# RWKV-7 units with two heads in turn on the array, and the latent outputs of both directions in one bank for each head

## The chip, the cores and the metric

The kernel runs on one core of a Trainium2 chip. The metric is the device time of one execution in microseconds: 2151.57 us as the median of three runs of the kernel before (2148.89 to 2158.67). A core has engines with instruction streams of their own: TensorE (PE, matrix products, with its weight loads as PEld), VectorE (DVE), ScalarE (ACT), GpSimd (POOL) and SyncE (SP, which issues most loads).

## The reference

Two layers of a hybrid backbone over 256 latent and 256 context tokens of width 1024. Layer 0 mixes with a gated linear recurrence beside windowed attention and has a dense feed-forward part. Layer 1 mixes with S5 (a complex diagonal state space model) beside RWKV-7 in both directions and ends in a choice of 2 of 8 experts. What the change touches is the RWKV-7 recurrence of layer 1, with 8 heads of 64:

```python
def _rwkv7_scan(r, w, k, v, a, b, s0):
    def step(s, inp):
        rt, wt, kt, vt, at, bt = inp
        sa = jnp.einsum('bhij,bhj->bhi', s, at)
        s = s * wt[:, :, None, :] + sa[..., None] * bt[:, :, None, :] + vt[..., None] * kt[:, :, None, :]
        return s, jnp.einsum('bhij,bhj->bhi', s, rt)
    ...
oc_f, sc_f = _rwkv7_scan(rc, dc[0][0], dc[0][1], vc, dc[0][2], dc[0][3], zero)
ol_f, _ = _rwkv7_scan(rl, dl[0][0], dl[0][1], vl, dl[0][2], dl[0][3], sc_f)
oc_b, sc_b = _rwkv7_scan(*[rev(t) for t in (rc, dc[1][0], dc[1][1], vc, dc[1][2], dc[1][3])], zero)
ol_b, _ = _rwkv7_scan(*[rev(t) for t in (rl, dl[1][0], dl[1][1], vl, dl[1][2], dl[1][3])], sc_b)
out_l = finish(ol_f + rev(ol_b), rl, kl, vl, gl)
```

Only the latent outputs are wanted in this layer; the context gives the state with which the latent tokens start.

## The kernel before

The recurrence is worked out in chunks of 64 tokens: four of context and four latent, in two directions. A unit is one chunk in one direction; step i (0 to 7) takes one unit of each direction d, by `SEQ`, and from step 4 on the chunks are latent. The eight heads lie as four pairs p, and within a pair head h takes the partitions 0 to 63 (h = 0) or 64 to 127 (h = 1): `h2(h)` is that slice. Products are small: 64 columns wide, over 64 or 128 rows.

`unit_before` (L1757) makes what of a unit doesn't need the state. It loads X (`uX`), and for latent chunks makes the gram product of each pair and head: 64 rows, 128 columns, four pairs of one head in one bank, two evacuations by VectorE with a mask (into `lk` and `uz`), then the same for the other head (L1782 to 1788). For context chunks the gram is 64x64 and the heads alternate already. `ztr` is a product with a diagonal matrix that gives the keys (`zh`).

`unit_inverse` (L1808) finishes the inverse of the unit's triangular matrix: two rounds of 32x32 products into one bank (`pi`), four pairs of head 0 and its evacuation (`uP`, `uY`), then four of head 1, in each round.

`rwkv_units` (L1830) runs the eight steps. In one step, for both directions: loads of v into the lower half of `vu` and of the state tile (L1873 and on); `pq`, the products of the gram with the state, whose heads alternate; `pz`, the inverse times `pq` (L1887 to 1892), four pairs of head 0 and then four of head 1, with ScalarE copying head 0's half and VectorE head 1's half into `vu`; `ph`, the new state (L1903 to 1909), again head after head, added to the decayed old state by VectorE (`uT`). Then `unit_inverse` of the next step. The outputs of a latent step are written one step later in `outputs` (L1848 to 1862): for each direction and head a bank `po`, and for each of four pairs a product `uz` x `vu` (128 rows) and one of `uRr` x `uT` (the old state, 64 rows) that adds to it; then one evacuation of 64x256 into `rO`, a copy by ScalarE or an addition by VectorE. `PLACE` says which half of the partitions of which of two output tiles a chunk belongs to; the two chunks of a step are always the two halves of one tile.

Beside this a generator of S5 is advanced twice for each step: its blocks of VectorE work (L1113 and on, L1392 to 1406) and its transposes and products on TensorE (`tp`) lie between the steps.

The order on each engine isn't written by hand: a tile scheduler sets it from the code's order and the buffers' dependences. While the units run, TensorE's results go to banks of PSUM by kind: `pq`, `pz` and `ph` turn through three, S5's `tp` through two, and `gram`, `ztr`, `pi` and `po` through three. After the units come `rwkv_finish`, the output projection, and from about 1340 us the experts.

Of the kernel before, what the change touches and what calls it, by code (L numbers as in the profile page):

```python
# [165 lines left out]
class Build:  # L166
# [1590 lines left out]
    def unit_before(self, i, d, rp, lk, zh, zp=None):  # L1757

        nc = self.nc
        V = nc.vector  # L1760
        tri = self.tri
        h2 = lambda h: slice(h * 64, h * 64 + 64)
        hi = h2(1)
        p128 = lambda n: self.psum_mx(n).rearrange("p (a b) -> p a b", a=4)
        ch = self.SEQ[d][i]
        lat = ch >= 4
        X = rp.tile([128, 4, 256], F32, name="uX", tag="uX", bufs=2)
        n = 256 if lat else 192
        nc.sync.dma_start(X[:, :, :n], self.d_x[d][ch][:, :, :n])

        if i:
            for h in range(2):
                nc.sync.dma_start(lk[h2(h), h], self.d_x[d][ch][h2(h), :, 128:192])
        bc = lambda ap: ap[:, None, :].to_broadcast([ap.shape[0], 4, 64])
        z = R = None
        if lat:
            t0 = (ch - 4) * 64
            r = self.r_r[:, :, t0:t0 + 64]
            R = zp.tile([128, 4, 64], F32, name="uRr", tag="uRr", bufs=6)
            nc.gpsimd.tensor_mul(R, X[:, :, 192:256], r)  # L1780
            nc.gpsimd.tensor_copy(X[:, :, 192:256], R)
            z = zp.tile([128, 4, 2, 64], F32, name="uz", tag="uz", bufs=6)  # L1782
            for h in range(2):
                pg = p128(f"gram{d}{i}")
                for p in range(4):
                    self.mm(pg[:, p], X[h2(h), p, 0:128], X[h2(h), p, 128:256], True, True)
                V.tensor_mul(lk[h2(1 - h), h], pg[hi, :, 0:64], bc(tri[hi, 0]))
                V.tensor_mul(z[:, :, h], pg[:, :, 64:128], bc(tri[:, 1 + d]))
        else:
            pg = p128(f"gram{d}{i}")[:, :, :64]  # L1790
            for p in range(4):
                for h in range(2):
                    self.mm(pg[h2(1 - h), p], X[h2(h), p, 64:128], X[h2(h), p, 128:192], True, True)
            for h in range(2):
                V.tensor_mul(lk[h2(1 - h), h], pg[h2(1 - h)], bc(tri[h2(1 - h), 0]))
        if i < 7:

            dl = rp.tile([128, 4, 128], F32, name="udl", tag="udl", bufs=1)
            dec = self.r_last[:, d, ch]
            nc.gpsimd.tensor_mul(dl, self.ident[:, None, :].to_broadcast([128, 4, 128]),  # L1800
                                 dec[:, :, None].to_broadcast([128, 4, 128]))
            pt = p128(f"ztr{d}{i}")
            for p in range(4):
                self.mm(pt[:, p], X[:, p, 0:128], dl[:, p], True, True)
            nc.scalar.copy(zh, pt)
        return lk, z, zh, R

    def unit_inverse(self, rp, i, d):  # L1808

        nc = self.nc  # L1810
        ch = self.SEQ[d][i]
        Y = rp.tile([128, 4, 64], F32, name="uY", tag="uY", bufs=4)
        W = rp.tile([128, 4, 32], F32, name="uW", tag="uW", bufs=2)
        nc.scalar.dma_start(W, self.d_w[d, ch].rearrange("i p t -> p i t"))
        nc.scalar.dma_start(Y, self.d_y[d, ch].rearrange("i p t -> p i t"))
        pi = self.psum_mx(f"pi{d}{i}")[:, :256].rearrange("p (n a b) -> p n a b", n=2, a=4)
        pb = rp.tile([128, 4, 32], F32, name="uP", tag="uP", bufs=2)
        for h in range(2):
            r, o = slice(h * 64 + 32, h * 64 + 64), slice(h * 64, h * 64 + 32)
            for p in range(4):  # L1820
                self.mm(pi[o, 0, p], W[r, p], Y[r, p, 32:64], True, True)
            self.evac(pb[o], pi[o, 0])
        for h in range(2):
            o = slice(h * 64, h * 64 + 32)
            for p in range(4):
                self.mm(pi[o, 1, p], W[o, p], pb[o, p], True, True)
            self.evac(Y[o, :, 32:64], pi[o, 1])
        return Y

    def rwkv_units(self, ra, rp, done, inv, room):  # L1830

        nc = self.nc
        V = nc.vector
        O = self.r_O = rp.tile([128, 2, 512], F32, name="rO", bufs=1)
        h2 = lambda h: slice(h * 64, h * 64 + 64)
        lo, hi = h2(0), h2(1)
        p64 = lambda n: self.psum_mm(n)[:, :256].rearrange("p (a b) -> p a b", b=64)
        heads = [(p, h) for p in range(4) for h in range(2)]
# [8 lines left out]

        def outputs(i, Ss, vus):  # L1848

            for d in range(2):  # L1850
                n, rows = self.PLACE[self.SEQ[d][i]]
                z, X, S, vu = before[i, d][1], before[i, d][3], Ss[d], vus[d]
                for h in range(2):
                    po = self.psum_mx(f"po{d}{i}")[:, :256].rearrange("p (a b) -> p a b", b=64)
                    for p in range(4):
                        self.mm(po[rows, p], z[:, p, h], vu[:, p, h], True, False)
                        self.mm(po[rows, p], X[h2(h), p], S[h2(h), h, p], False, True)
                    o = O[rows, n].rearrange("p (a h v) -> p a h v", a=4, h=2)[:, :, h]
                    if (d == 0) == (self.SEQ[d][i] < 6):
                        nc.scalar.copy(o, po[rows])  # L1860
                    else:
                        V.tensor_add(o, o, po[rows])

        left = None
        for i in range(8):
            last, lat = i == 7, i >= 4
            vus, Rs, Ss = [], [], list(state)
            for d in range(2):

                ch, S = self.SEQ[d][i], state[d]  # L1870
                vu = rp.tile([128, 4, 2, 64], F32, name="vu", tag="vu", bufs=4)
                dv = self.d_v[d][ch * 64:ch * 64 + 64].rearrange("t (p h v) -> t p h v", p=4, h=2)
                nc.sync.dma_start(vu[hi], dv)  # L1873
                for h in range(2):
                    nc.sync.dma_start(S[h2(1 - h), h], dv[:, :, h])
                vus.append(vu)

            for d in range(2):
                lk, S = before[i, d][0], state[d]
                pq = p64(f"pq{d}{i}")  # L1880
                for p, h in heads:
                    r = slice(0, 128) if i else h2(1 - h)
                    self.mm(pq[h2(h), p], lk[r, h, p], S[r, h, p], True, True)
                R = rp.tile([128, 4, 64], F32, name="uR", tag="uR", bufs=2)
                nc.scalar.copy(R, pq)
                Rs.append(R)
            for d in range(2):  # L1887
                pz = p64(f"pz{d}{i}")
                for h in range(2):
                    for p in range(4):  # L1890
                        self.mm(pz[h2(h), p], inv[i, d][h2(h), p], Rs[d][h2(h), p], True, True)
                    (V.tensor_copy if h else nc.scalar.copy)(vus[d][lo, :, h], pz[h2(h)])
            if not last:
                for d in range(2):
                    zh, S, dec = before[i, d][2], state[d], self.r_last[:, d, self.SEQ[d][i]]
                    ph = p64(f"ph{d}{i}")
                    N = new_state()
                    t = None
                    if i:
                        t = rp.tile([128, 4, 64], F32, name="ulT", tag="ulT", bufs=2)  # L1900
                        for h in range(2):
                            nc.gpsimd.tensor_mul(t[h2(h)], S[h2(h), h], dec[h2(h), :, None].to_broadcast([64, 4, 64]))
                    for h in range(2):  # L1903
                        for p in range(4):
                            self.mm(ph[h2(h), p], zh[:, p, h2(h)], vus[d][:, p, h], True, True)
                        if i:
                            V.tensor_add(N[h2(h), h], t[h2(h)], ph[h2(h)])
                        else:
                            (V.tensor_copy if h else nc.scalar.copy)(N[h2(h), h], ph[h2(h)])
                    state[d] = N  # L1910
                for d in range(2):
                    inv[i + 1, d] = self.unit_inverse(rp, i + 1, d)
            if left:
                outputs(*left)
            left = (i, Ss, vus) if lat else None
            if i < 3:
                ahead(2 * i + 6, 2 * i + 8)
            if i in (4, 5):
                ahead(2 * i + 4, 2 * i + 6)
            yield  # L1920
# [404 lines left out]
```

## Time and profile before

| | |
|---|---|
| median of the runs | 2151.57 us |
| the profiled execution | 2162.4 us |
| its span, first to last instruction | 2160.6 us |
| mean granted TensorE clock | 0.930 of 2.4 GHz |
| TensorE busy | 2019.5 us, 93% of the span |
| VectorE busy | 1624.6 us, 75% |
| ScalarE busy | 1048.2 us, 49% |
| GpSimd busy | 176.3 us, 8% |
| the units on TensorE | about 1037 to 1257.8 us |

All later readings are of the profiled execution. TensorE's busy time is the union of its instructions from their start to their modelled end, so records that overlap count once. An fp32 product of the code leaves two records. The granted clock has two levels, 1.2 GHz (0.50) and 2.4 GHz (1.00).

### The profile page before, as it was taken

The page shows a single profiled execution, that of the slowest core. Times are in us where ns is not written, and L with a number is a line of the kernel's source. Part 1 is how long each engine was busy: PE and PEld are TensorE (multiplying, and loading weights), DVE is VectorE, ACT ScalarE, POOL GpSimd, SP SyncE. Part 2 cuts the span into 40 slices and gives each one's busy share as a digit, 9 for nine tenths or more (in the row PEclk, how much of TensorE's full clock was granted, in tenths as well). Part 3 has the DMA queues.
Part 4 walks back from the last instruction along what each step waited for, and adds up shares of the span by engine and source line. Part 5 has one row for each costly group of instructions (what it writes and reads, how often), then busy time and mean ns, then how long its engine had stood idle before and what let it go on. Part 6 is the DMA issues. An engine that isn't in the chain of part 4 may idle for free. (4 is left out here: it accounts for less than half of the span.)

```text
span 2160.6 us, 31186 instructions
## 1 busy us (share of the span) xinstructions
PE 2019.5 (93%) x11518; PEld 1591.5 (74%) x11518; DVE 1624.6 (75%) x3051; ACT 1048.2 (49%) x1604; POOL 176.3 (8%) x222
## 2 busy tenths in 40 slices
PE   7999999999999997895799979999999999999994
PEld 4766777777888876583688857788887777777773
DVE  3566756798777687877554287898989888888886
ACT  3334434332333335651222236777767777677762
POOL 1000000001000011004441033000000000000000
PEclk9999999999999999896666578999999999999997
DMA  8434223347566563477762175999989899998890
GB/s 301 124 109 147 80 78 97 130 151 231 197 195 192 152 169 126 141 226 240 194 177 76 32 267 202 359 344 354 348 328 341 328 346 327 347 331 333 325 357 21
DMA packets 148756, 476.66 MB, mean 221 GB/s; under 512 B 54020, under 2 KB 72532, under 8 KB 113524
## 3 DMA queue, kind: packets, MB, share of 16 engines
q1 hardware_dynamic: 120610, 428.13, 56.4%
q0 software_dynamic: 9648, 34.93, 5.1%
q10 hardware_dynamic: 18338, 11.54, 1.9%
q8 instruction: 92, 1.51, 0.3%
q14 instruction: 68, 0.56, 0.1%
HBM read 442.56 MB, written 31.98 MB: 220 GB/s over the span
## 5 line engine op out<-in xcount | busy, mean ns | idle before, releaser
L201 DVE TENSOR_TENSOR mwl<-mraw,mwh 128x1024 fp32r<-128x1024 f32 x522 | 617.7, 1231 | 57.1 <-ACT mwh L197 52.6
L197 ACT CAST mwh<-mraw 128x1024 fp32r<-128x1024 f32 x528 | 520.3, 1051 | 56.1 <-PE mm L179 32.2
L179 PE MATMUL mm<-hh,wl 128*128 128x512 f32 (+1 forms) x744 | 284.7, 384 | 7.8 <-DVE wl L201 7.8
L179 PE MATMUL mm<-hl,wh 128*128 128x512 f32 (+1 forms) x744 | 286.4, 386 | 4.4 <-DVE hl L452 4.4
L179 PE MATMUL mm<-hh,wh 128*128 128x512 f32 (+1 forms) x744 | 285.9, 387 | 2.7 <-ACT hh L451 2.3
L197 ACT CAST wh<-wraw 128x1024 fp32r<-128x1024 f32 x119 | 124.8, 1050 | 318.3 <-PE mm L179 243.8
L201 DVE TENSOR_TENSOR wl<-wraw,wh 128x1024 fp32r<-128x1024 f32 x119 | 145.1, 1220 | 85.8 <-ACT wh L197 79.5
L179 PE MATMUL mm<-mwh,hgh 128*128 128x512 f32 (+1 forms) x768 | 196.0, 377 | 4.1 <-ACT mwh L197 4.0
L179 PE MATMUL mm<-mwl,hgh 128*128 128x512 f32 (+1 forms) x768 | 196.7, 378 | 2.4 <-DVE mwl L201 2.4
L179 PE MATMUL mm<-mwh,hgl 128*128 128x512 f32 (+1 forms) x768 | 195.7, 377 | 0.0
L179 PEld LDWEIGHTS mm<-hh,wl 128*128 128x128 f32 x744 | 142.9, 192 | 36.7 <-DVE wl L201 9.2
L179 PEld LDWEIGHTS mm<-hh,wh 128*128 128x128 f32 x744 | 141.6, 191 | 34.3 <-ACT wh L197 4.4
L179 PEld LDWEIGHTS mm<-hl,wh 128*128 128x128 f32 x744 | 142.7, 192 | 31.8 <-DVE hl L452 4.8
L179 PEld LDWEIGHTS mm<-mwh,hgh 128*128 128x128 f32 x768 | 136.7, 188 | 34.9 <-ACT mwh L197 5.8
L179 PEld LDWEIGHTS mm<-mwl,hgh 128*128 128x128 f32 x768 | 136.0, 189 | 35.1 <-DVE mwl L201 7.3
L179 PEld LDWEIGHTS mm<-mwh,hgl 128*128 128x128 f32 x768 | 136.6, 188 | 28.6
L179 PE MATMUL mx<-mwh,mah 128*128 128x512 f32 x352 | 103.4, 402 | 1.1 <-ACT mwh L197 1.1
L179 PE MATMUL mx<-mwh,mal 128*128 128x512 f32 x352 | 104.0, 401 | 0.0
L179 PE MATMUL mx<-mwl,mah 128*128 128x512 f32 x352 | 99.8, 399 | 0.0
L179 PEld LDWEIGHTS mx<-mwh,mah 128*128 128x128 f32 x352 | 64.2, 188 | 20.4 <-ACT mwh L197 7.4
L179 PEld LDWEIGHTS mx<-mwl,mah 128*128 128x128 f32 x352 | 65.3, 188 | 14.1
L179 PEld LDWEIGHTS mx<-mwh,mal 128*128 128x128 f32 x352 | 64.7, 188 | 13.4
(600 smaller groups left out, 3283.6 us busy)
## 6 DMA issues: line engine op xcount, KB each, us to landing
mraw<-in_moe_w_dram SPq DMA_DIRECT2D x264, 1024.0 KB, 6.0
adaw<-in_ada_w_dram SPq DMA_DIRECT2D x96, 512.0 KB, 4.9
wraw<-in_ev_w_in_dram SPq DMA_DIRECT2D x26, 512.0 KB, 3.7
wraw<-in_ffn_w_gate_dram SPq DMA_DIRECT2D x22, 512.0 KB, 4.4
wraw<-in_ffn_w_up_dram SPq DMA_DIRECT2D x22, 512.0 KB, 4.4
wraw<-in_ffn_w_down_dram SPq DMA_DIRECT2D x22, 512.0 KB, 4.1
wraw<-in_od_w_in_dram SPq DMA_DIRECT2D x19, 512.0 KB, 4.0
d5ca<-ca POOLq DMA_DIRECT2D x32, 144.0 KB, 4.0
```

What stands on the lines that cost most here:

```text
L179: self.nc.tensor.matmul(out, lhsT, rhs, start=start, stop=stop, skip_group_check=True)
L197: self.nc.scalar.copy(hi, raw)
L201: self.nc.vector.tensor_sub(lo, raw, hi.bitcast(F32))
```

## The change

In `unit_before`, `unit_inverse`, `pz` and `ph` the loops over pairs and heads are exchanged: a product of head 0, the same of head 1, and so on; the evacuations follow after both. The latent gram therefore takes two banks before its first product, one for each head. `outputs` is written anew: a bank for each head that holds both directions, in the partition halves that `PLACE` gives; first all `uz` x `vu` of pairs and directions, the directions in turn, then all `uRr` x `uT` added to them; then an evacuation of 128x256 for each head. The number of products is the same. For the outputs of the four latent steps there are 8 evacuations of 128x256 instead of 16 of 64x256.

```diff
--- before.py
+++ after.py
@@ -1780,10 +1780,11 @@
             nc.gpsimd.tensor_mul(R, X[:, :, 192:256], r)
             nc.gpsimd.tensor_copy(X[:, :, 192:256], R)
             z = zp.tile([128, 4, 2, 64], F32, name="uz", tag="uz", bufs=6)
-            for h in range(2):
-                pg = p128(f"gram{d}{i}")
-                for p in range(4):
-                    self.mm(pg[:, p], X[h2(h), p, 0:128], X[h2(h), p, 128:256], True, True)
+            pgs = [p128(f"gram{d}{i}") for _ in range(2)]
+            for p in range(4):
+                for h in range(2):
+                    self.mm(pgs[h][:, p], X[h2(h), p, 0:128], X[h2(h), p, 128:256], True, True)
+            for h, pg in enumerate(pgs):
                 V.tensor_mul(lk[h2(1 - h), h], pg[hi, :, 0:64], bc(tri[hi, 0]))
                 V.tensor_mul(z[:, :, h], pg[:, :, 64:128], bc(tri[:, 1 + d]))
         else:
@@ -1815,16 +1816,18 @@
         nc.scalar.dma_start(Y, self.d_y[d, ch].rearrange("i p t -> p i t"))
         pi = self.psum_mx(f"pi{d}{i}")[:, :256].rearrange("p (n a b) -> p n a b", n=2, a=4)
         pb = rp.tile([128, 4, 32], F32, name="uP", tag="uP", bufs=2)
+
+        r, o = ([slice(h * 64 + s, h * 64 + s + 32) for h in range(2)] for s in (32, 0))
+        for p in range(4):
+            for h in range(2):
+                self.mm(pi[o[h], 0, p], W[r[h], p], Y[r[h], p, 32:64], True, True)
         for h in range(2):
-            r, o = slice(h * 64 + 32, h * 64 + 64), slice(h * 64, h * 64 + 32)
-            for p in range(4):
-                self.mm(pi[o, 0, p], W[r, p], Y[r, p, 32:64], True, True)
-            self.evac(pb[o], pi[o, 0])
+            self.evac(pb[o[h]], pi[o[h], 0])
+        for p in range(4):
+            for h in range(2):
+                self.mm(pi[o[h], 1, p], W[o[h], p], pb[o[h], p], True, True)
         for h in range(2):
-            o = slice(h * 64, h * 64 + 32)
-            for p in range(4):
-                self.mm(pi[o, 1, p], W[o, p], pb[o, p], True, True)
-            self.evac(Y[o, :, 32:64], pi[o, 1])
+            self.evac(Y[o[h], :, 32:64], pi[o[h], 1])
         return Y
 
     def rwkv_units(self, ra, rp, done, inv, room):
@@ -1847,19 +1850,22 @@
 
         def outputs(i, Ss, vus):
 
-            for d in range(2):
-                n, rows = self.PLACE[self.SEQ[d][i]]
-                z, X, S, vu = before[i, d][1], before[i, d][3], Ss[d], vus[d]
-                for h in range(2):
-                    po = self.psum_mx(f"po{d}{i}")[:, :256].rearrange("p (a b) -> p a b", b=64)
-                    for p in range(4):
-                        self.mm(po[rows, p], z[:, p, h], vu[:, p, h], True, False)
-                        self.mm(po[rows, p], X[h2(h), p], S[h2(h), h, p], False, True)
-                    o = O[rows, n].rearrange("p (a h v) -> p a h v", a=4, h=2)[:, :, h]
-                    if (d == 0) == (self.SEQ[d][i] < 6):
-                        nc.scalar.copy(o, po[rows])
-                    else:
-                        V.tensor_add(o, o, po[rows])
+            po = [self.psum_mx(f"po{i}{h}")[:, :256].rearrange("p (a v) -> p a v", a=4) for h in range(2)]
+            where = [self.PLACE[self.SEQ[d][i]] for d in range(2)]
+            n = where[0][0]
+            assert where[1][0] == n
+
+            for k in range(2):
+                for p, h in heads:
+                    for d, (_, rows) in enumerate(where):
+                        l, r = ((before[i, d][1][:, p, h], vus[d][:, p, h]), (before[i, d][3][h2(h), p], Ss[d][h2(h), h, p]))[k]
+                        self.mm(po[h][rows, p], l, r, k == 0 and p == 0, k == 1)
+            for h in range(2):
+                o = O[:, n].rearrange("p (a h v) -> p a h v", a=4, h=2)[:, :, h]
+                if i < 6:
+                    nc.scalar.copy(o, po[h])
+                else:
+                    V.tensor_add(o, o, po[h])
 
         left = None
         for i in range(8):
@@ -1886,9 +1892,9 @@
                 Rs.append(R)
             for d in range(2):
                 pz = p64(f"pz{d}{i}")
+                for p, h in heads:
+                    self.mm(pz[h2(h), p], inv[i, d][h2(h), p], Rs[d][h2(h), p], True, True)
                 for h in range(2):
-                    for p in range(4):
-                        self.mm(pz[h2(h), p], inv[i, d][h2(h), p], Rs[d][h2(h), p], True, True)
                     (V.tensor_copy if h else nc.scalar.copy)(vus[d][lo, :, h], pz[h2(h)])
             if not last:
                 for d in range(2):
@@ -1900,9 +1906,9 @@
                         t = rp.tile([128, 4, 64], F32, name="ulT", tag="ulT", bufs=2)
                         for h in range(2):
                             nc.gpsimd.tensor_mul(t[h2(h)], S[h2(h), h], dec[h2(h), :, None].to_broadcast([64, 4, 64]))
+                    for p, h in heads:
+                        self.mm(ph[h2(h), p], zh[:, p, h2(h)], vus[d][:, p, h], True, True)
                     for h in range(2):
-                        for p in range(4):
-                            self.mm(ph[h2(h), p], zh[:, p, h2(h)], vus[d][:, p, h], True, True)
                         if i:
                             V.tensor_add(N[h2(h), h], t[h2(h)], ph[h2(h)])
                         else:
```

On TensorE in step 0, from the first `pz` on (names: out<-moving,stationary inputs with buffer numbers; the digits behind pz, ph, pi, gram are direction and step; xN is a run of N products), before:

```order
L179 MATMUL pz10_9727<-uR_9714,uY_9367 64x64 x3
L179 MATMUL pz00_9716<-uR_9703,uY_9341 64x64 x4
L179 MATMUL pz10_9727<-uR_9714,uY_9367 64x64
L179 MATMUL ph00_9738<-vu_9686,zh_9039 64x64 x4
L179 MATMUL pi01_9766<-uY_9762,uW_9763 32x32 x2
L179 MATMUL gram03_9818<-uX_9814 64x64 x4
L179 MATMUL pi11_9792<-uY_9788,uW_9789 32x32 x4
L179 MATMUL pz10_9727<-uR_9714,uY_9367 64x64 x4
```

and in the changed kernel:

```order
L179 MATMUL pz00_9716<-uR_9703,uY_9341 64x64 x8
L179 MATMUL pz10_9727<-uR_9714,uY_9367 64x64 x8
L179 MATMUL ph00_9738<-vu_9686,zh_9039 64x64
L179 MATMUL pi01_9766<-uY_9762,uW_9763 32x32 x5
L179 MATMUL pi11_9792<-uY_9788,uW_9789 32x32 x8
L179 MATMUL gram03_9818<-uX_9814 64x64 x6
L179 MATMUL tp_9873<-U_9864,wb5_9862 64x64 x16
L179 MATMUL tp_9663<-ca5_9605,xs_9616 32x128 x8
L179 MATMUL ph00_9738<-vu_9686,zh_9039 64x64 x7
```

Each `pz` is now one run of eight, and of `ph` only the first product stands before the `pi`, gram and S5 products, the other seven behind them; before, four stood ahead and four behind.

On TensorE where the outputs of step 4 are made (`po` with direction, step before; step, head in the changed kernel), before:

```order
L179 MATMUL po04_11142<-vu_10720,uz_10091 64x64
L179 MATMUL po04_11142<-uT_10563,uRr_10088 64x64
L179 MATMUL mm_11233<-yh5_9600,gwh_11236 128x256
L179 MATMUL mm_11233<-yl5_9601,gwh_11236 128x256
L179 MATMUL pi06_11094<-uP_11095,uW_11091 32x32 x4
L179 MATMUL po14_11162<-vu_10724,uz_10123 64x64
L179 MATMUL po14_11162<-uT_10578,uRr_10120 64x64
```

and in the changed kernel:

```order
L179 MATMUL po40_11142<-vu_10720,uz_10091 64x64
L179 MATMUL ph05_11060<-vu_11008,zh_10357 64x64 x7
L179 MATMUL ph15_11075<-vu_11012,zh_10389 64x64 x5
L183 MATMUL tp_10993<-ident_73,y5_10702 128x32 x8
L179 MATMUL ph15_11075<-vu_11012,zh_10389 64x64 x3
L179 MATMUL pi06_11094<-uP_11095,uW_11091 32x32 x8
L179 MATMUL po40_11142<-vu_10724,uz_10123 64x64
L179 MATMUL po40_11142<-uT_10563,uRr_10088 64x64
L179 MATMUL pi16_11120<-uP_11121,uW_11117 32x32 x8
L179 MATMUL po40_11142<-uT_10578,uRr_10120 64x64
```

A product with `vu` no longer stands before each product with `uT`: those with `vu` of the head come first, the two directions' buffers in turn, and `pi` stands in runs of eight.

## Rows read from the trace of the kernel before

**Rows 1.** Busy time in stretches: us, busy (instructions) of each engine, TensorE's clock, DMA.

```profile
1037.00:1163.50 126.50, 123.14 (x1520) 102.89 (x1518) 76.59 (x206) 29.39 (x91) 48.93 (x68) 0.69 0.61 156
1163.50:1257.80 94.30, 93.28 (x676) 73.69 (x674) 33.13 (x96) 19.75 (x51) 10.82 (x17) 0.60 0.22 62
...
1340.00:2160.00 820.00, 783.72 (x3640) 629.38 (x3638) 713.94 (x740) 563.46 (x647) 2.52 (x2) 0.99 0.85 321
```

**Rows 2.** TensorE's waits, 1037 to 1257.8: us in total, times, longest.

```profile
PE pi L179 <- DMA uY<-dry: 1.6, 1, 1.6
```

**Rows 3.** Stretches, po on TensorE alone: busy (records), clock, DMA.

```profile
1163.50:1257.80 94.30, 46.34 (x256) 0.60 0.22 62
```

**Rows 4.** The same view, pz.

```profile
1037.00:1163.50 126.50, 16.93 (x192) 0.69 0.61 156
```

**Rows 5.** The same view, ph.

```profile
1037.00:1163.50 126.50, 18.06 (x168) 0.69 0.61 156
```

**Rows 6.** The same view, gram.

```profile
1037.00:1163.50 126.50, 20.43 (x128) 0.69 0.61 156
```

**Rows 7.** The same view, pi.

```profile
1037.00:1163.50 126.50, 25.53 (x397) 0.69 0.61 156
```

**Rows 8.** The tile vu: record lengths in ns (min/median/max), loads to landing.

```profile
L179 PE MATMUL ph<-vu,zh x176: 221/313/370, 1055.3 to 1209.1; 128*64 128x64 f32 x176
...
DMA to landing us min/median/max: 2.4/3.2/8.1
```

**Rows 9.** Timeline of TensorE, several stretches: start, us, operation, xrecords.

```profile
1056.66 0.69 PE L179 MATMUL gram<-uX 64*64 64x64 f32 x8
...
1068.52 0.69 PE L179 MATMUL pq<-uT,lk 128*64 128x64 f32 x16
...
1091.77 3.09 PE L179 MATMUL gram<-uX 64*128 64x128 f32 x16
...
1165.09 0.63 PE L179 MATMUL ph<-vu,zh 128*64 128x64 f32 x8
...
1167.03 1.97 PE L179 MATMUL ph<-vu,zh 128*64 128x64 f32 x16
...
1178.33 0.63 PE L179 MATMUL pi<-uP,uW 32*32 32x32 f32 x8
...
1179.29 0.47 PE L179 MATMUL po<-vu,uz 128*64 128x64 f32 x2
1179.69 0.47 PE L179 MATMUL po<-uT,uRr 64*64 64x64 f32 x2
...
1184.10 5.17 PE L179 MATMUL gram<-uX 64*128 64x128 f32 x32
...
1195.94 1.33 PE L179 MATMUL pq<-uT,lk 128*64 128x64 f32 x18
```

**Rows 10.** Stretches, TensorE alone: us, busy (records), granted clock, DMA.

```profile
1056.60:1057.40 0.80, 0.80 (x13) 0.50 0.86 148
1066.00:1069.00 3.00, 3.00 (x72) 1.00 0.99 281
1091.80:1094.80 3.00, 3.00 (x18) 0.50 0.60 193
1165.00:1165.70 0.70, 0.70 (x11) 1.00 0.90 143
1167.00:1197.00 30.00, 30.00 (x216) 0.50 0.16 41
```

**Rows 11.** Timeline of VectorE: an S5 block's first and last row, then vu.

```profile
1069.01 0.42 DVE L1113 TENSOR_TENSOR rt<-E,tp 128x256 f32<-128x256 f32 x1
...
1077.27 0.22 DVE L1406 TENSOR_TENSOR xs<-rt,rt 64x64 f32<-64x64 f32 x1
1077.52 0.77 DVE L1892 COPY vu<-pz 64x256 f32<-64x256 f32 x2
```

**Rows 12.** SyncE's waits, 1150 to 1420: us in total, times, longest.

```profile
SPq L1873 <- PE po L179: 35.1, 4, 22.7
```

## The prediction

> **What bounds the kernel now.** I read the busy time by stage first [rows 1]. From 1037 to 1257.8 us, where the units run, TensorE is busy 123.14 of 126.5 us and then 93.28 of 94.3; VectorE, ScalarE and GpSimd have far more idle time. The waits of TensorE in the same stretch come to little: the longest is 1.6 us, for a load [rows 2]. So TensorE sets this stage, and what leaves its stream can leave the time. What follows does not absorb a shift: from 1340 us on TensorE is busy 783.72 of 820 us at a clock of 0.99 [rows 1], on the experts, whose instructions the change leaves alone. A stage that ends 10 us sooner should end the kernel 10 us sooner.
>
> The clock is not full here: 0.69 of 2.4 GHz in the first part and 0.60 in the second [rows 1]. With two levels, 1.2 and 2.4 GHz, a mean of 0.69 is 62% of the time at the lower one, and 0.60 is 80%.
>
> Then the busy time of the products that the change touches. The latent outputs, po, are the largest: 46.34 us for 256 records, all in the second part [rows 3]. (A record is one pass of the array; an fp32 product in the code leaves two.) In the first part pz takes 16.93 us (192 records), ph 18.06 (168), gram 20.43 (128, of which 96 are the 64x128 form of the later units), pi 25.53 (397) [rows 4 to 7].
>
> **What one record costs, in a row of one head and in turn.** A group's time on the timeline is its records' pitch plus the last record's own length, 0.37 us at the low clock and 0.22 at the full one (the extremes of ph in [rows 8]). Sixteen ph of one head after the other take 1.97 us at a granted clock of 0.50 [rows 9, 10]: (1.97 - 0.37) / 15 = 0.107 us each. The eighteen pq from 1195.94 us, whose heads already take turns, take 1.33 us at 0.50: 0.96 / 9 = 0.107 us for a pair, 0.053 a record. At a clock of 1.00, eight ph take 0.63 us, 0.059 each, and sixteen pq 0.69 us, 0.059 for a pair [rows 9, 10]. So two heads that take turns run together, and the second one is free: a 64-wide record that gets a partner saves 0.0535 us at the low clock, 0.0295 at the full one. Weighted with the shares of the clock, that is 0.044 in the first part and 0.049 in the second (0.62 x 0.0535 + 0.38 x 0.0295; 0.80 and 0.20).
>
> **The outputs.** Today z·vu uses the whole array's rows and X·S half of them, and they alternate. Two records start every 0.40 us at the low clock (1179.29, 1179.69) [rows 9, 10], 0.20 a record, nearly twice the 0.107 of records of one shape, so each change of shape costs about 0.09. Over the whole part a record costs 46.34 / 256 = 0.181 us [rows 3]. The change puts all z·vu of a head before all X·S, and lets the two directions (two column halves) alternate: half the pitch of one head, 0.049 a record. 256 x (0.181 - 0.049) = 33.8 us, less the changes of shape that stay (two heads, four steps, two at each, 16 x 0.09) 1.4: **32.4 us**. Their evacuations become 8 of 128x256 instead of 16 of 64x256; half as many instructions of the same 256 columns. ScalarE and VectorE are busy 19.75 and 33.13 of the 94.3 us [rows 1], so I cost the difference at nothing; if they were the bound, it would be a gain.
>
> **The other products in the second part.** pz 64 records x 0.049 = 3.1 us; ph 56 x 0.049 = 2.7. Counts of the second part are 256 - 192 and 224 - 168, since each step has the same number and the last has no ph. Gram: 32 records take 5.17 us [rows 9], 0.16 each, because the end of one head already runs beside the start of the next; a pair that alternates takes 2 x 0.107 (twice the width), so 0.053 is saved, 1.7 us. pi is half as wide, so I take half the prices of a 64-wide record, 0.053 at the low clock (eight take 0.63 us [rows 9], which leaves 0.26 for the last one's own length), and a saving of 0.024: 0.024 x 116 = 2.8. With the outputs: 32.4 + 3.1 + 2.7 + 1.7 + 2.8 = **42.7 us**.
>
> **The first part.** ph 168 x 0.044 = 7.5 us. Gram, 96 of the wide form: about 0.18 today by the 16 that take 3.09 us at the low clock [rows 9, 10] (0.19 each with the last one's own length), against 0.107, and less at the full one, so 0.06: 5.8 us. pi 397 x 0.022 = 8.7. pz 192 x 0.044 = 8.5, but I count this at nothing: the copies of pz into vu on VectorE start the moment the S5 block before them ends (1077.27 + 0.22 against 1077.52) [rows 11], so an earlier pz finds VectorE busy, and ph, the state and the next step's pq follow from that copy. It is worth 8.5 again if VectorE is free by then. Of the other 22.0 us I take nine tenths, **20 us**: TensorE is the bound by [rows 1], but VectorE is busy 76.59 of the 126.5 us, so some of the freed time will be a wait for it. The bounds are 0 (the S5 block sets the pace of a step; a rival below) and 22.0.
>
> **What is given back.** A step's vu goes into a buffer that the outputs of two steps before must have read: SyncE stands 35.1 us for po, four times [rows 12], and a vu takes 3.2 us to land [rows 8]. Today this is covered by the time that TensorE needs for a step. In the new order the z·vu of both directions come before any X·S, so the old states, which wait for the last X·S, and vu come free close together at the end of a step that is now shorter. I count one load in the open for steps 6 and 7: 2 x 3.2 = 6.4 us, from bounds of 0 and four loads (12.8).
>
> The gram needs two banks at once in place of one after the other. The pool of three banks turns as before, the total of banks asked for is the same, and for the outputs it falls from 16 to 8; I cost this at nothing, and at 1.7 us (the second part's gram) if the second bank is late.
>
> Sum: 20 + 42.7 - 6.4 = **56.3 us**. The profiled span of 2160.6 us becomes 2104.3; the profiled run stands at 2162.4, 10.8 above the median of the runs, 2151.57. The same 56.3 off the median is 2095.3: **2095 us**.
>
> **The rivals.**
> *TensorE alone sets the stage*: pz counts too, nothing is given back, all of 8.5 + 22.0 + 42.7 = 73 us goes: 2078.5 us. For it: the waits of [rows 2]. Against: [rows 11].
> *VectorE holds the first part*: the S5 block stands ahead of the copies of each step, and nothing of the first part's 20 us comes: 36 us, 2115.5. For it: the S5 generator is advanced twice in each step; against: VectorE is idle 40% there.
> *Row halves into one bank do not overlap*: pi and pz take a row half for each head, and both heads write one bank. If such records had to wait for each other, they would save nothing: 56.3 - 0.9 x 8.7 - 3.1 - 2.8 = 42.6 us, 2109. Against it: the 64x64 grams of the early units do just that, both row halves into one bank, and eight of them take 0.69 us at the low clock [rows 9, 10], where eight in turn would take 0.37 + 7 x 0.107 = 1.12.
> The Trainium skill, "TensorEngine Tiling (Array Packing)", section "Gotcha 1: PSUM Pressure", says that different row tiles cannot access the same PSUM bank at the same time, which is this rival. By that rule the time is the rival's 2109; by the 0.69 us it is the forecast's, and I go by the row.
> *Slower*: with the heads in turn, the second product of ph needs the half of vu that VectorE copies behind the S5 block; before, four products of head 0 could run on ScalarE's copy alone. If TensorE stands for a block's 8.5 us (1069.01 to 1077.49 [rows 11]) in each of six steps, that is 51 us; and if it stands so much that the clock stays at 1.2 GHz, the rest of the first part, 123 - 31 = 92 us, grows by 0.69 / 0.5, +35, and the second's 51 by 0.60 / 0.5, +10. 51 + 45 against 73 - 6.4 freed: 29 us more, 2181. It decides from 22 us of standing (3.6 a step) if the clock goes, and from 67 (11 a step) if it does not. Against it: the built order sets other products (pi, gram, the S5 transposes) between ph's first and the rest, so there is work to stand in.
> *The heads alternate in the code but the hardware gains nothing*, since something else spaces the records: about 2151.5. The pq of today speak against it.
>
> **How the numbers follow.** Forecast 0.59 (its own range 2085 to 2106: a load more or less, the first part's share between seven tenths and all); TensorE alone 0.15; VectorE holds 0.14; one bank 0.05; slower 0.04; nothing 0.03. The range goes from 2070 (TensorE alone, and fewer changes of shape between pi and others give 8 us more) to 2120 (VectorE holds, with another 4.5 given back). What this kernel's runs can tell from no change is about 0.5%, 10.8 us: faster 0.93, the same 0.03, slower 0.04.
>
> **What would show it.** Right: po near 12 us of records' pitch (256 x 0.049), two records every 0.107 us at the low clock; pz, ph and pi in pairs; the stage's end near 1201 us instead of 1257.8; VectorE's copies of vu still with no idle time before them. The first part shorter by about 20 us and the second by 36. Wrong: TensorE's waits in the stage far above a few us, on VectorE (vu, uT) or on vu's load; a clock lower than 0.6 through the stage; records of pi or pz that still start 0.054 and 0.107 us apart; or a TensorE gap after the stage that was not there, which would mean that the experts' loads, not the stage, set their start.

## The result, and the profile after

The changed kernel takes 2089.61 us (median of 4 runs, 2082.49 to 2095.13) beside 2155.12 us of the kernel before in the same series: a ratio of 0.9692, with a 95% interval of 0.9639 to 0.9744, some 66 us less. A second series on another occasion gave 0.9688 (0.9640 to 0.9736). The prediction said 2095, between 2070 and 2120, from a gain of 56.3 us.

| | before | after |
|---|---|---|
| span of the profiled execution, us | 2160.6 | 2080.7 |
| mean granted clock | 0.930 | 0.955 |
| TensorE busy, us | 2019.5 | 1926.7 |
| VectorE busy, us | 1624.6 | 1622.7 |

The two profiled executions lie 79.9 us apart, more than the medians. Executions of one kernel differ with their clock: the kernel before took 2165.55 us in a run with a mean clock of 0.929 and 2144.16 in one with 0.940. So the medians say what the change is worth, and the profiles say where.

I cut the stage where most of step 0's `pq` begin (six records stand earlier before the change and two after it, from 1037.0 and 1035.7 us on), at the first `pq` of step 5 and at the last `po`. First the busy time in these stretches before, and then after (columns: stretch, length, busy time and instructions of PE, PEld, DVE, ACT and POOL, granted clock, DMA share, GB/s):

```profile
1050.70:1151.50 100.80, 99.34 (x1223) 82.58 (x1219) 63.46 (x168) 23.09 (x70) 43.51 (x62) 0.68 0.65 167
1151.50:1257.70 106.20, 105.18 (x841) 83.76 (x838) 42.95 (x126) 23.05 (x60) 14.23 (x22) 0.65 0.25 70
```

```profile
1046.90:1128.80 81.90, 73.14 (x1251) 59.39 (x1248) 63.92 (x173) 23.38 (x72) 43.52 (x64) 0.80 0.79 206
1128.80:1182.10 53.30, 47.07 (x807) 39.31 (x803) 41.00 (x126) 19.80 (x53) 13.76 (x20) 0.91 0.45 127
```

Steps 0 to 4 are 18.9 us shorter, steps 5 to 7 with the last outputs 52.9; the stage starts 3.8 us earlier, and what comes after the last `po` takes 898.6 us where it took 902.9. Nothing behind the stage took the gain back. Two things besides the length changed. TensorE is no longer full: idle for 8.8 us of the first part and 6.2 of the second, where it had been 1.5 and 1.0. And the clock is higher in both.

TensorE's waits between 1046.9 and 1182.1 us (total, times, longest), where [rows 2] stood before:

```profile
PE tp L179 <- DVE xs L1406: 4.6, 7, 1.2
PE pq L179 <- DVE z L1396: 2.3, 1, 2.3
PE mm L179 <- issue: 1.7, 1, 1.7
PE pi L179 <- DMA uW<-drw: 1.4, 1, 1.4
PE gram L179 <- POOL uX L1781: 0.9, 1, 0.9
```

They are small and of several kinds. The view lists 14.0 us in all: 6.9 are for S5's VectorE work (xs, z), the rest is for loads, GpSimd and copies. None is for `vu` or its load. SyncE's wait for `po` before that load, 35.1 us in [rows 12], is now:

```profile
SPq L1879 <- PE po L179: 9.9, 3, 4.9
```

The products in pairs, on TensorE's timeline (start, us, operation, records):

```profile
1049.40 1.97 PE L179 MATMUL pz<-uR,uY 64*64 64x64 f32 x32
...
1166.28 1.15 PE L179 MATMUL pz<-uR,uY 64*64 64x64 f32 x32
1167.36 0.45 PE L179 MATMUL po<-vu,uz 128*64 128x64 f32 x8
1167.74 0.69 PE L179 MATMUL po<-uT,uRr 64*64 64x64 f32 x32
```

and the clock there:

```profile
1049.40:1051.30 1.90, 1.90 (x34) 0.50 0.77 163
1158.00:1160.00 2.00, 1.47 (x57) 1.00 0.03 8
1166.00:1169.00 3.00, 2.44 (x84) 1.00 0.10 12
```

At the low clock 32 records of `pz` take what 16 of `ph` in a row took in [rows 9], 1.97 us: two heads for the price of one. The last line is better than a pair; it comes back below. All of `po`, by stretch (length, busy and records, clock, DMA), against 46.34 us in [rows 3]:

```profile
1128.80:1182.10 53.30, 11.68 (x256) 0.91 0.45 127
```

### The profile page after: what moved, and what is told of

Read it like the earlier page. It is cut to its first block, busy times and chain, and to the rows that moved or that the text cites. A ratio compares the mean times of both kernels' runs of the same rounds, so it can differ in the third digit from the quotient of the medians.

```text
span 2080.7 us, 31160 instructions
## 1 busy us (share of the span) xinstructions
PE 1926.7 (93%) x11518; PEld 1515.0 (73%) x11518; DVE 1622.7 (78%) x3047; ACT 1045.9 (50%) x1600; POOL 175.5 (8%) x222
## 5 line engine op out<-in xcount | busy, mean ns | idle before, releaser
L201 DVE TENSOR_TENSOR mwl<-mraw,mwh 128x1024 fp32r<-128x1024 f32 x522 | 617.6, 1232 | 56.3 <-ACT mwh L197 51.8
```

The costliest lines, as they stand in the source:

```text
L201: self.nc.vector.tensor_sub(lo, raw, hi.bitcast(F32))
```

## The experiments

**The two halves of the change.** First the outputs alone: the kernel before with `outputs` as in the diff, everything else as it was.

> The kernel before with only the outputs rewritten; gram, pi, pz and ph stay head after head. Theory (each record saves its pitch at the clock that the stage had): about 32 us less than before, ratio 0.985, all of it after the fifth pq; the granted clock of 1163 us and on stays near 0.60. Rival (the denser outputs also bring the clock back): 45 us or more, ratio 0.979 or lower, with a granted clock over 0.75 in the second part and the first part as before. Second rival (the outputs give more only if the other products are paired too): under 25 us.

Measured: ratio 0.9846 (0.9811 to 0.9881), 33 us of 2149, as the first theory had it in time. But the clock of the profiled execution did rise, in the second part alone, as the rival had it. Steps 0 to 4, then 5 to 7, of this kernel:

```profile
1037.60:1139.50 101.90, 100.46 (x1223) 83.38 (x1219) 63.85 (x169) 23.15 (x70) 44.42 (x63) 0.67 0.64 165
1139.50:1203.10 63.60, 59.93 (x840) 50.90 (x836) 41.22 (x129) 20.17 (x55) 13.87 (x21) 0.89 0.39 101
```

The first part is that of the kernel before; TensorE is as full as it was and the clock as low. The second is 42.6 us shorter than in the profile of before. The 33 us of the runs are less: the profile of before is one of its slower executions (2162.4 us), this one of the faster of its kernel (2107.9, median 2116.18).

Then everything but the outputs: the changed kernel with `outputs` as before.

> The changed kernel with the outputs as they were. Theory (terms add up): first part 19 to 20 us shorter, second part about 10, 30 us in all, ratio 0.986; po stays at about 46 us. Rival (VectorE's S5 block holds the first part): 10 us, ratio 0.995. Rival (the clock rises with the pairs): 30 us in the first part alone and a granted clock of 0.8 there. With the first experiment this tells whether the two halves of the change add up to the whole, 0.969.

Measured: 0.9849 (0.9816 to 0.9881), 32.5 us. Its parts:

```profile
1047.50:1129.80 82.30, 75.05 (x1297) 61.24 (x1294) 67.06 (x182) 24.01 (x73) 45.98 (x66) 0.84 0.83 211
1129.80:1210.40 80.60, 78.74 (x760) 61.50 (x760) 38.27 (x112) 20.78 (x56) 11.33 (x17) 0.72 0.30 85
```

The first part has the changed kernel's length and clock, the second lies between. The halves add up: 33 + 32.5 = 65.5 us, the whole is 66 to 67.

**What of the outputs is the pair, and what the change of shape.** Two ways to write them that keep one bank for each head. In the first the directions don't take turns:

```diff
-            for k in range(2):
-                for p, h in heads:
+            for h in range(2):
+                for k in range(2):
                     for d, (_, rows) in enumerate(where):
...
+                        for p in range(4):
```

> The changed kernel, but in the outputs the two directions no longer take turns: for a head four products of one direction, then four of the other, first all uz x vu, then all uRr x uT. Theory (the pair gives half the pitch): po goes from 11.7 to about 20 us of busy time and the time is 8 to 12 us over that of the changed kernel, ratio to before 0.973 to 0.975. Rival (the changes of shape were the whole cost of the outputs): within 3 us of the changed kernel, 0.969 or 0.970.

In the second the directions take turns, and the two products of a pair follow each other:

```diff
+            for h in range(2):
+                for p in range(4):
+                    for k in range(2):
                         for d, (_, rows) in enumerate(where):
```

> The changed kernel, but in the outputs the uRr x uT of a pair follow its uz x vu at once, with the directions in turn: 64 changes of shape instead of 16. Theory (a change of shape costs 0.05 to 0.09 us): 3 to 5 us over the changed kernel, po about 17 us of busy time, ratio 0.970 to 0.972. Rival (a change of shape keeps the next pair from running together and costs a whole pitch or more): 10 us or more, 0.974.

Measured, grouped: 0.9725 (0.9689 to 0.9760); pair by pair: 0.9744 (0.9709 to 0.9779). Against 0.9688 for the changed kernel that is 8 and 12 us. The intervals are some 8 us to either side of each and 10 us for the changed kernel, so the runs alone don't tell either from nothing; the busy time does. `po` alone from 1130 to 1260 us, for the changed kernel, grouped, and pair by pair:

```profile
1130.00:1260.00 130.00, 11.71 (x256) 0.87 0.55 198
```

```profile
1130.00:1260.00 130.00, 17.47 (x256) 0.85 0.54 184
```

```profile
1130.00:1260.00 130.00, 21.94 (x256) 0.76 0.49 173
```

So 5.8 and 10.2 us more of busy time, about what the ratios say. Steps 5 to 7 of the grouped kernel stand at a clock of 0.92 (length, busy of the engines, clock as above):

```profile
1138.30:1193.60 55.30, 49.76 (x800) 42.62 (x796) 39.92 (x125) 19.61 (x53) 13.80 (x20) 0.92 0.44 116
```

At that clock the pitch of one head is 0.16 x 0.107 + 0.84 x 0.059 = 0.067 us, and 17.47 / 256 = 0.068: grouped, the records run one after the other with few changes of shape. So of the 34.6 us that `po` lost (46.34 to 11.71) the turns of the directions have 5.8, and the shapes and the clock the rest. At the clock of before, 0.65, the same 256 records would take about 24 us (0.7 x 0.107 + 0.3 x 0.059 = 0.093 each), so the shapes have about 22 of it and the clock some 6, an estimate.

Pair by pair, 48 more changes of shape cost 10.2 us, 0.21 each at most (the clock of this execution was lower too, and no four products go together any more, below): the rival's size, and more than the 0.05 to 0.09 of the theory. The theory's price was misread from [rows 9]. The 0.40 us there are two records of one product and one change, so a change cost 0.40 - 2 x 0.107 = 0.19 us at the low clock. At the full one it is less. Pair by pair, groups of four records start 0.26 us apart at a granted clock of 1.00 (1160.8 to 1164.6 us), where two pairs need 2 x 0.059: 0.15 us a change.

```profile
1161.11 0.34 PE L179 MATMUL po<-vu,uz 128*64 128x64 f32 x4
1161.38 0.33 PE L179 MATMUL po<-uT,uRr 64*64 64x64 f32 x4
1161.64 0.34 PE L179 MATMUL po<-vu,uz 128*64 128x64 f32 x4
```

The alternating outputs also add to a bank that was written just before, and that could be the cost instead. No such addition is needed: in step 0 of the changed kernel two records of `ph` stand between `pz` and `pi`, nothing there adds to an earlier product, and at a clock of 0.50 the next shape again starts 0.40 us later.

```profile
1051.31 0.47 PE L179 MATMUL ph<-vu,zh 128*64 128x64 f32 x2
1051.71 0.95 PE L179 MATMUL pi<-uY,uW 32*32 32x32 f32 x26
```

**Each product undone.** Four kernels, each the changed one with one product put back to head after head, and the changed kernel itself in the series of `pz` and `ph`:

> The changed kernel as it is, on the chip of the runs beside it, to compare them with it directly. Expected: ratio to before 0.969 as measured already, 2083 to 2095 us. If outputs alone (0.985) and the rest alone (0.985) add up without anything beyond, it is 0.970.

> The changed kernel with pz head after head again. Theory of the prediction (pz of the first part lies under VectorE's S5 block): 2 to 3 us over the changed kernel, which these runs can hardly tell from none. Rival (TensorE alone sets the stage, pz counts in full): 9 to 12 us.

> The changed kernel with ph head after head again, each head's addition right behind its four products. Theory (ph costs TensorE its pitch): 7 to 10 us over the changed kernel. Rival (head 0 of ph can start on ScalarE's half of vu, so the old order has an earlier start that the new one gave up): no more than 2 us over, or faster.

> The changed kernel with pi head after head again, each head's copy behind its four products. By the prediction's price (8.7 x 0.9 + 2.8 us at the clock of before): 8 to 11 us over the changed kernel, ratio to before 0.973 to 0.974 where the changed one had 0.969. Rival (pi's records ran beside each other already where two directions met, and the changed kernel has idle TensorE time to spare): under 4 us.

> The changed kernel with the latent gram head after head again, one bank at a time. By the prediction's price (5.8 x 0.9 + 1.7 us): 4 to 7 us over the changed kernel, 0.971 to 0.972. Rival (asking for two banks at once costs what the pairs give): within 2 us, or faster.

The edits are the diff's own pieces turned round, as here for `pz`:

```diff
-                for p, h in heads:
-                    self.mm(pz[h2(h), p], inv[i, d][h2(h), p], Rs[d][h2(h), p], True, True)
                 for h in range(2):
+                    for p in range(4):
+                        self.mm(pz[h2(h), p], inv[i, d][h2(h), p], Rs[d][h2(h), p], True, True)
```

The difference to the changed kernel's 0.9688, times 2153 us:

| undone | ratio to before | 95% interval | us over the changed kernel | price in the prediction, us |
|---|---|---|---|---|
| nothing | 0.9688 | 0.9640 to 0.9736 | | |
| outputs (the run above) | 0.9849 | 0.9816 to 0.9881 | 34.7 | 32.4 |
| pz | 0.9762 | 0.9706 to 0.9819 | 15.9 | 3.1 |
| ph | 0.9740 | 0.9691 to 0.9788 | 11.2 | 9.5 |
| pi | 0.9726 | 0.9678 to 0.9774 | 8.2 | 10.6 |
| gram | 0.9684 | 0.9643 to 0.9725 | -0.9 | 6.9 |

The five add up to 69 us, the whole to 67. An interval is about 10 us to either side, so by the ratios only the outputs are clear of it by far. Beside kernels of their own series more can be told. The changed kernel's median there is 2080.68 us and its slowest run 2090.53; `pz` undone has 2098.56, with five of six runs above that slowest one, `ph` undone 2094.92, with four of six. `pi` undone has 2094.97, and five of six runs lie above the slowest of `gram` undone (median 2085.37, slowest 2086.89). So `pz`, `ph` and `pi` each count; `ph` and `pi` came out near their prices, `pz` above and `gram` below. The scheduler orders each of these kernels anew, so more than the named loop can differ.

For `pz` the busy time says more than the runs do. With `pz` undone, steps 0 to 4 and 5 to 7, and below it the changed kernel (length, busy and records of `pz`, clock, DMA):

```profile
1050.30:1139.40 89.10, 15.65 (x160) 0.83 0.76 196
1139.40:1192.80 53.40, 7.77 (x96) 0.87 0.39 106
```

```profile
1046.90:1128.80 81.90, 9.26 (x160) 0.80 0.79 206
1128.80:1182.10 53.30, 3.66 (x96) 0.91 0.45 127
```

10.5 us of TensorE's time, and the last `po` ends 10.7 us later (1192.8 against 1182.1; 1178.2 in a second execution of the changed kernel). The gain on `pz` was not hidden. The lengths of the stage say less: it takes 135.2 us in one execution of the changed kernel and 145.1 in the other, which starts it 13.8 us earlier.

For `gram`, undone and then in the changed kernel, 1030 to 1200 us:

```profile
1030.00:1200.00 170.00, 20.25 (x160) 0.82 0.67 177
```

```profile
1030.00:1200.00 170.00, 17.89 (x160) 0.81 0.65 177
```

The difference is 2.4 us of TensorE's time, and that is not shown to be the order: a second execution of the changed kernel has 21.48 us in the same stretch, at a clock of 0.79. At the higher clock the grams are cheap, and head after head they ran beside each other in part already, as 0.16 us a record in [rows 9] had shown.

**Who waits for VectorE.** Two kernels ask whether the S5 blocks on VectorE set the pace, as the prediction's step on `pz` supposed. The first takes the copies of `vu` away from VectorE:

```diff
-                    (V.tensor_copy if h else nc.scalar.copy)(vus[d][lo, :, h], pz[h2(h)])
+                    nc.scalar.copy(vus[d][lo, :, h], pz[h2(h)])
```

> The changed kernel with both halves of vu copied by ScalarE, so that no copy stands behind VectorE's S5 block. Theory (the copies of vu wait for the S5 block and hold the steps of the first part): the first part, 82 us from the second pq to the sixth, gets 5 us or more shorter and the time 5 to 15 us. Rival (TensorE has enough other work there): within 3 us of the changed kernel.

Measured: 0.9720 (0.9673 to 0.9767), not faster; the point lies 7 us over the changed kernel, within the intervals, and the first part of the profile is 90.4 us long, at a clock of 0.75, not shorter than 82. The second takes VectorE's work itself away, in the changed kernel and in the one before:

```diff
         e.tensor_mul(t1, ar, br)
         e.tensor_mul(t2, ai, bi)
+        if half:
+            return t1, t2, t1, t2
         e.tensor_mul(t3, ar, bi)
```

> The changed kernel with two of the four products left out in each of S5's two complex multiplications (the first two stand in for them), which takes about 1.3 us of VectorE work out of each of eight blocks; S5's result is not what it should be, the rest is whole. Theory (after the change VectorE's S5 work sets a part of the first part's pace: TensorE is idle 8.8 of its 81.9 us): 5 to 9 us under the changed kernel, ratio to before 0.965 to 0.966. Rival (TensorE's idle time has other reasons, and TensorE still sets the pace): within 2 us, 0.968 to 0.970.

> The kernel before with the same products of S5 left out. Theory (TensorE was busy 99.34 of 100.8 us there, so VectorE's work was all covered): within 3 us of the kernel before, ratio 0.999 to 1.000. Rival (the copies of vu behind the S5 block held the steps already before the change, as the prediction's step on pz had it): 5 us or more under it, 0.997 or lower.

Measured: 0.9728 (0.9686 to 0.9769) in the changed kernel, 1.0013 (0.9982 to 1.0045) in the kernel before. The edit removed 32 instructions but less time than I had put down, since neighbours on VectorE overlap: busy time fell from 1622.7 to 1618.5 us after and from 1624.6 to 1619.0 before. Before, this is what a full TensorE predicts.

After, the kernel is no faster: the point lies some 9 us over the changed kernel, and six of seven runs over the slowest one of `gram` undone in the same series. But this run doesn't settle the question. The scheduler built another order for it: 1291 of TensorE's records stand before step 5, where the changed kernel has 1251. In that order TensorE waits for VectorE, longest for the copies of `vu`. First steps 0 to 4, then two of TensorE's waits up to the last `po`:

```profile
1034.20:1128.90 94.70, 83.90 (x1291) 68.60 (x1288) 67.57 (x163) 24.33 (x74) 46.09 (x66) 0.74 0.74 184
```

```profile
PE ph L179 <- DVE vu L1900: 7.1, 3, 3.8
PE tp L179 <- DVE xs L1408: 3.8, 7, 0.8
```

So these two runs neither support nor exclude the theory that VectorE's S5 blocks hold the first part; 4 us less work is little, and the order changed with it. Of TensorE's 15 us of idle time in the changed kernel about half, 6.9 us, is put down to S5's VectorE work (xs and z, above); what a kernel without those waits would gain is open.

## Why the prediction was right, and where its steps were not

The time, 2089.61, lies 5 us under the 2095 that was forecast, and near the middle of the range. The gain was farther off, 66 us against 56.3: the kernel before took 2155.12 us in this series, 3.6 more than the median from which the forecast was taken. That TensorE's time sets the stage, and that neighbours in turn run together, was right. That the sum came so close is in part luck, as several of its terms were off and the clock, which is not in it, rose. The steps, one by one:

**TensorE bounds the stage before.** Held: less VectorE work did nothing there (1.0013), and all but one of the pieces that took time from TensorE moved the total.

**The price of a pair.** Held: 1.97 us for 32 records of `pz` at the low clock, 1.15 us at the full one, (1.15 - 0.22) / 16 = 0.058 us a pair.

**The outputs, 32.4 us.** 33 us when done alone and 34.7 when undone. Two errors in it were small: a change of shape costs 0.19 us and not 0.09, so the 16 that stay should have been 3.0 us and not 1.4, and the second products run four at a time in part (below), not two. The busy time of `po`, 11.7 us where about 12 were the sign of being right, is partly luck: the 12 are pairs at the old clock, and at 0.91 the same pairs take 256 x 0.034 = 8.6 us, to which the dearer changes of shape add 2.4 to 3.0.

**ph and pi.** 9.5 and 10.6 forecast, 11.2 and 8.2 measured by the undoing, inside the intervals.

**pz at nothing in the first part.** This step failed. I had looked at the chain through one `vu`, found it behind a VectorE block, and concluded that a sooner `pz` gives nothing. What I saw was there: the copies still start at a block's end in four of the six steps that have one, in step 0 for example, as the timeline of VectorE after the change shows:

```profile
1057.77 0.22 DVE L1406 TENSOR_TENSOR xs<-rt,rt 64x64 f32<-64x64 f32 x1
1058.02 0.77 DVE L1898 COPY vu<-pz 64x256 f32<-64x256 f32 x2
```

But on a full engine the time that `pz` gives up is used by whatever stands next in its queue, whether or not somebody waits for `pz`. And the block doesn't run at a pace of its own: it needs TensorE's products. In the kernel before, VectorE idled 1.76 us for `tp` ahead of one:

```profile
1097.52 0.42 DVE L1113 TENSOR_TENSOR rt<-E,tp 128x256 f32<-128x256 f32 x1 [1.76 <-PE tp L179]
```

The term should have been counted in full, 8.5 us more. `pz` undone cost 15.9 us by the ratios, where the step allowed 3.1; that a sooner `tp` is how the gain came through is argued, not shown.

**gram, 6.9 us.** Too large: undoing it costs nothing that can be measured, and the 2.4 us of TensorE's time are less than two executions of one kernel differ by (17.89 and 21.48). I had priced it at the low clock of 1092 us, and that clock did not stay.

**What is given back, 6.4 us for loads of vu.** The place was wrong: no wait of TensorE in the stage is for `vu` or its load. The size was too small: TensorE's idle time in the stage grew by 7.3 + 5.2 = 12.5 us, over many small waits, where the sum had 6.4 and the tenth of the first part, 2. So pairs alone, 73 us, less 12.5, is 60.5 of the 66 measured. The errors on `pz` (8.5 too little gain), `gram` (some 4.5 too much) and the idle time (some 4 too much) nearly cancel, and the 10 us by which the forecast's gain is short are left to the clock (next).

**The clock.** Not in the sum at all. In steps 5 to 7 it went from 0.65 to 0.91. That this alone shortens products is seen on `pq`, whose heads took turns before already and which the change leaves alone: over the stage, before and after (length, busy and records, clock, DMA),

```profile
1050.70:1257.70 207.00, 16.44 (x250) 0.66 0.45 117
```

```profile
1046.90:1182.10 135.20, 12.95 (x254) 0.84 0.65 175
```

What the clock is worth can be bounded from two executions of the changed kernel: with 0.91 these steps took 53.3 us, and in the second series' profile, with 0.77, 59.2.

```profile
1119.00:1178.20 59.20, 53.95 (x807) 45.66 (x803) 41.15 (x127) 19.93 (x53) 14.42 (x21) 0.77 0.42 116
```

5.9 us for 0.14, so some 11 us for 0.26, an estimate in proportion. Of the 52.9 us that the profiles show there, about 42 are then left for the products; the forecast for its second part was 42.7, and 36.3 with the loads. The clock rose in the part whose products had been paired: the second alone when the outputs were changed (0.67 and 0.89), and more in the first when everything else was (0.84 and 0.72). That is one execution each, and the clock of one kernel varies (0.77 and 0.91 above), so that the change brought the clock back is likely, not shown. What the engine must do for it stays open: the stretches at 0.50 before [rows 10] held long rows of products of one head and outputs in alternating shapes, but also grams whose heads take turns (1056.6 us), and the paired `pz` at 1049.4 us of the changed kernel stood at 0.50 too.

**The rivals.** TensorE alone (2078.5) came closer than I had given it: the gain of 66 us lies nearer its 73 than the forecast's 56.3, and two of its terms, `pz` and no wait for loads of `vu`, were right. VectorE holding the first part fell, since that part is 18.9 us shorter. So did the slower rival: `ph` waits for nothing long. Its mechanism exists, though: the 7.1 us for `vu` in the run with less S5 work are that wait. And row halves into one bank do run together: `pz` writes both heads into one bank, and 32 records take 0.93 us between the first and the last start at a clock of 1.00, half of what 32 in a row would need at 0.059. The rule in the Trainium skill, "TensorEngine Tiling (Array Packing)", "Gotcha 1: PSUM Pressure", that different row tiles cannot access the same PSUM bank at the same time, does not hold for these products; the measurement decides.

## What to carry to other kernels

On an engine that is full for a whole stage, price every piece of time that leaves its queue, also that of a product nobody waits for, and then subtract the idle time that will appear; don't follow one product's chain. Small products that use half of the array's rows or columns cost half when neighbours in the queue use the other half, and products of different shapes that alternate pay 0.15 to 0.2 us at each change here, so sort by shape first and alternate halves second. A stage at a low clock is not a fixed price list: here the granted clock of steps 5 to 7 went from 0.65 to 0.91, and a term priced at the old clock (`gram`) came out too large. And a run that takes work out of one engine also gets a new order from the scheduler; read its waits before you draw a conclusion from its time.

## What the hardware showed that I had not expected

**Four products at once.** In the changed outputs the `uRr` x `uT` products use 64 rows (a head) and 64 columns (a direction), and where both heads' banks are free the order has all four combinations in turn. The last line of the first TensorE timeline above: 32 records in 0.69 us at a clock of 1.00. Less the last one's 0.22, that is 0.47 us for eight groups of four, 0.059 a group: four records for the price of one, where the prediction had two. The Trainium skill, "TensorEngine Tiling (Array Packing)", "Available Configurations", lists four tiles for the 64x64 mode, and the trace agrees with 0.059 us for four.

**Records that overlap without turns.** The grams of before, head after head, took 0.16 us a record at a clock of 0.50 [rows 9, 10], where 0.214 (twice the 0.107 of a record half as wide) is the pitch of one head: the end of one head's run went beside the start of the next. Part of what the pairs promised was there already.
